# A hybrid decoder layer: where two of the five sums of output-weight quarters are made, and the ticks that space the others

## The chip, the cores and the metric

The program runs on one core of one Trainium2 chip. The metric is the device time of one execution in microseconds, taken as the median of several runs. All data is float32; every large product is made of three TensorE matmuls, because each operand is split into a high part (rounded to float32r) and a low part (the rest).

## What is computed

One decoder layer on 1024 positions of width 2048, cut to the parts that matter here:

```python
xn = rms_norm(x, norm_w)
proj = xn @ w_in                      # 2048 x 7184, cut into head groups A and B
o_a = group_a(proj)                   # gated delta rule, 8 heads of 128
o_b = u_b * chunked_causal_sgu(layer_norm(v_b), w_s, b_s) * silu(z_b)   # 8 groups of 128
mix = concatenate([o_a, o_b]) @ w_out # 2048 x 2048
out = rms_norm(x + mix, final_norm_w)
```

## The kernel before

**Stages.** The 1024 positions are worked in two halves of 512. For each half comes group A (projections, convolution, and the recurrence in pairs of heads) and then group B: three blocks of the v projection (`vb`), and then sixteen projections of 128 columns, u and z in turn. A projection is four loads of `w_in` (tile `wr`, 256 KB each), each split by ScalarE (`wh`, line 135) and VectorE (`wl`, line 136), and 48 matmuls into `acc` (lines 237, 238 and 240). After both halves comes the output phase.

**The output phase** makes the last product with seven block products in place of eight (Strassen's scheme): the table `PRODUCTS` gives for each of the seven the quarters of the mixed activations that are added, the quarters of `w_out` that are added, and the blocks of the result that it goes into. Each product has two column halves (`cb`) of eight steps `k`; a step has one weight tile `wro` of 256 KB (split into `who`, `wlo`) and twelve matmuls into `oa` (lines 970 to 972). With `cb` 0 a step also loads and splits the activations (`ar` or `as`, then `a`). At the end of each column half, VectorE adds four accumulators into one or two result blocks each (line 908, `c`); the first time that a block is written it adds the residual `xres`, which is loaded into the tile tag `z` (two buffers).

**The sums.** Five of the seven products (0, 2, 3, 4 and 6) need a sum or a difference of two quarters of `w_out`. `w_sums` (line 828 on) makes them during group B, 80 units of 128 by 512, 40 in each half. A unit loads two tiles (`wsa`, `wsb`, lines 834 and 835; tags `cv` with three buffers and `bv` with two), adds them on VectorE (line 842) and stores the sum in DRAM through POOL's queue (`wc_d`, line 843). The output phase later loads `wro` from `wc_d`, for products 1 and 5 from `w_out` itself.

**What sets the order.** A list of tasks (Python generators) is stepped by `tick()`, two ticks per load of `w_in`; each `yield n` waits n ticks. `run` holds four weight tiles prepared ahead. The framework then lays out each engine's instructions when the program is built: a row can stand before others that were written earlier. Loads and most stores are issued by SP in that fixed order, and an issue whose buffer isn't free holds all behind it. `swap` for the output of a head (`nc.gpsimd`) goes through POOL's queue: four stores (`swapo`, line 429), then one load back (`ut`, line 432), on which VectorE waits in line 671 (`o`).

Constants that the change touches: `W_SWO` (ticks between the swap of a pair's output and line 671), `W_SUM0` (ticks before the first unit), and the number in `w_sums`' `yield 3`.

Of the kernel before, what the change touches and what calls it, by code (L numbers as in the profile page):

```python
# [8 lines left out]
F32 = mybir.dt.float32  # L9
# [8 lines left out]
P = 128  # L18
DM = 2048
SEQ = 1024  # L20
T = 512
NHALF = SEQ // T
KT = DM // P
# [8 lines left out]
def kernel(ctx, tc, x_tok, x_t, w_in, w_v0, w_vb, w_out, conv_w, norm_w, a_log, dt_bias,  # L32
                       hn_w, sgu_w, sgu_b, wsp_t, b_sp, fn_w, out):
    nc = tc.nc
# [5 lines left out]
    wk = pool("wk", bufs=2)  # L40
    sm = pool("sm", bufs=2)
    dr = pool("dr", bufs=2, space=DRAM)
# [72 lines left out]
    tt = cst.tile([P, 2 * NT, P], F32, name="tt")  # L115
    nc.gpsimd.memset(tt, 0.0)

    wc_d = dr.tile([5, 2, KT // 2, P, T], F32, name="wc_d", bufs=1)
    mix_d = [dr.tile([2 * H, P, T], F32, name=f"mix_d{i}", bufs=1) for i in range(NHALF)]


# [11 lines left out]
    def split(hi, lo, src):  # L133

        nc.scalar.copy(hi, src)  # L135
        nc.vector.tensor_tensor(lo, src, hi.bitcast(F32), op=ALU.subtract)  # L136
# [43 lines left out]
        nc.scalar.copy(rb, rp)  # L180
        return rb

    def w_chunk(src, shape, name, keep=None, raw=None):
        if raw is None:
            raw = wp.tile(shape, F32, tag="wr", bufs=3, name=f"wr{name}")
        nc.sync.dma_start(raw, src)
        hi, lo = keep or (wp.tile(shape, F32R, tag="wh", name=f"wh{name}"), wp.tile(shape, F32R, tag="wl", name=f"wl{name}"))
        split(hi, lo, raw)
        return hi, lo
# [7 lines left out]
    def spawn(gen):  # L197
        n = next(gen, None)
        if n is not None:
            tasks.append([n, gen])  # L200
# [29 lines left out]
    def w_tile(hf, ct, q):  # L230
        return w_chunk(w_in[ct, :, q * KH:(q + 1) * KH, :], [P, KH, P], f"{hf}_{ct}_{q}")
# [29 lines left out]
    def first_tiles(hf, xs, env, done):  # L261
# [3 lines left out]
        for q in range(KT // 2):  # L265
            def prep(q=q):
                ks = slice(2 * q, 2 * q + 2)
                raw = wp.tile([P, 2, 2, P], F32, tag="wr", bufs=3, name=f"wrf{hf}_{q}")
                hi = wp.tile([P, 2, 2, P], F32R, tag="wh", name=f"whf{hf}_{q}")
                lo = wp.tile([P, 2, 2, P], F32R, tag="wl", name=f"wlf{hf}_{q}")  # L270
                sqs_, sqs[:] = list(sqs), []
                for i in range(2):
                    x, sq = x_load(hf, 2 * q + i)
                    xs.append(x)
                    sqs.append(sq)
                    nc.sync.dma_start(raw[:, i], w_in[(H, 0)[i], :, ks, :])
                    split(hi[:, i], lo[:, i], raw[:, i])
                if q % 3 == 0:
                    vraw.append(big.tile([P, 3, 2, 288], F32, tag="b8", name=f"v0r{hf}_{q}"))
                v2 = big.tile([P, 2, 2, 288], F32R, tag="b8", name=f"v0{hf}_{q}")[:, :, :, 0:V0]  # L280
                vb = w_chunk(w_v0[q], None, None, (v2[:, 0], v2[:, 1]), vraw[-1][:, q % 3, :, 0:V0])
                for sq in sqs_ + (sqs if q == KT // 2 - 1 else []):
                    sq()
                if hf == 0 and q == 5:
                    conv_constants()
                return hi, lo, vb
# [154 lines left out]
        return s4  # L441


    W_SWO = 20
    W_SO0 = 4
    W_CONV = 7
    W_SWAP = 7
# [6 lines left out]
    W_GATES = 12  # L454
    W_LN = 12
    W_EM = 5
    W_SUM0 = 30

    def task_k(hf, h, st, pr, acc):
        gt, hh = st["gt"], h % 2  # L460
# [87 lines left out]
    def task_pair(hf, p, st, pr):  # L548
# [95 lines left out]
        for h2, hd in enumerate(heads):  # L644
# [19 lines left out]
            yield 1  # L664
        yield W_SWO
        while not all("z" in hd for hd in heads):
# [100 lines left out]
    def group_b(hf, xs, st):  # L767

        env, sb = {}, {}
        units = [(n, cb, k) for n in SUMS for cb in range(2) for k in range(HK)]  # L770
        spawn(w_sums(units[hf * len(units) // 2:(hf + 1) * len(units) // 2]))
        for blk in range(1, 4):
            for k2 in range(KT // 2):
# [34 lines left out]
    PRODUCTS = (  # L808
# [7 lines left out]
    )  # L816
    SUMS = [n for n, pr in enumerate(PRODUCTS) if len(pr[1]) > 1]
    KEPT = ((0, 0), (1, 1))
    ASLOTS = [tb for tag, bufs in (("kd", 3), ("gae", 3), ("wq", 2), ("bv", 2), ("o", 2), ("ut", 2), ("kc", 2))
              for tb in [(tag, bufs)] * bufs]  # L820
    op = {1: ALU.add, -1: ALU.subtract}

    def w_quarter(b, cb, k):

        return w_out[b[1] * 2 + cb, b[0] * HK + k]

    def w_sums(units):

        def load(u):
            n, cb, k = u  # L830
            a, b, _ = PRODUCTS[n][1]
            ta = wk.tile([P, 1, T], F32, tag="cv", bufs=3, name=f"wsa{n}_{cb}_{k}")
            tb = wk.tile([P, 1, T], F32, tag="bv", bufs=2, name=f"wsb{n}_{cb}_{k}")
            nc.sync.dma_start(ta, w_quarter(a, cb, k))
            nc.sync.dma_start(tb, w_quarter(b, cb, k))
            return ta, tb
        yield W_SUM0
        nxt = load(units[0])
        for i, (n, cb, k) in enumerate(units):
            (ta, tb), nxt = nxt, (load(units[i + 1]) if i + 1 < len(units) else None)  # L840
            yield 3
            nc.vector.tensor_tensor(ta, ta, tb, op=op[PRODUCTS[n][1][2]])  # L842
            nc.gpsimd.dma_start(wc_d[SUMS.index(n), cb, k], ta.rearrange("p o c -> p (o c)"))

    def out_phase():
# [29 lines left out]
        def a_prep(n, k):  # L875
            spec = PRODUCTS[n][0]
            src = a_raw(n, spec[0], k)
            if len(spec) > 1:
                dst = src if spec[0] not in KEPT else wk.tile([P, T], F32, tag="cv", bufs=3, name=f"as{n}_{k}")
                nc.vector.tensor_tensor(dst, src, a_raw(n, spec[1], k), op=op[spec[2]])  # L880
                src = dst
            hi, lo = (wk.tile([P, T], F32R, tag=tag, bufs=bufs, name=f"a{i}{n}_{k}")
                      for i, (tag, bufs) in enumerate(ASLOTS[2 * k:2 * k + 2]))
            split(hi, lo, src)
            return hi, lo

        def prep(n, cb, k):
            src = w_quarter(PRODUCTS[n][1][0], cb, k) if n not in SUMS else \
                wc_d[SUMS.index(n), cb, k].rearrange("p (o c) -> p o c", o=1)
            keep = None  # L890
            if n == LAST and cb == 1 and k < HK - 4:
                keep = [act.tile([P, 1, T], F32R, tag="ah", name=f"wk{i}_{k}") for i in range(2)]
            w = w_chunk(src, [P, 1, T], f"o{n}_{cb}_{k}", keep)
            if cb == 0:
                return w, a_prep(n, k)
            return w, None
# [153 lines left out]
```

## Time and profile before

| | |
|---|---|
| median of 3 runs | 1821.09 us (1820.3 to 1825.88) |
| the profiled execution | 1825.52 us, its span 1823.4 us |
| mean granted TensorE clock | 0.989 |
| PE busy | 1739.9 us, 95% |
| VectorE (DVE) busy | 1267.0 us, 69% |
| ScalarE (ACT) busy | 733.3 us, 40% |
| group B, sixteen projections | 536.3 to 754 us, and 1287.1 to 1504.4 us |
| output phase | 1504.4 to 1823.4 us |

The profile is one execution. Busy time of PE counts a matmul at whatever clock it ran, so a stretch can be fully busy and still be slow; the granted clock stands beside it in the views by stretch. The difference of 2.1 us between the execution's time and its span lies outside the program's instructions.

### The profile page before, as it was taken

Reading aid. Unit: us, or ns where it says so; the run is one execution under the profiler, and the core shown is the slowest. Engines: PE = TensorE matmul, PEld = TensorE weight load, DVE = VectorE, ACT = ScalarE, POOL = GpSimd, SP = SyncE. Lnnn points to the kernel's source line nnn. Section 1 sums busy time; section 2 is a strip of 40 time slices with the busy share of each in tenths; the row PEclk is TensorE's granted clock in tenths of the full one; section 3 lists DMA queues with packets and bytes.
Section 4 is the critical chain, followed back from the end, with each engine's and each line's share of the span. In section 5 each row is a group of like instructions: output and inputs, shape, how many; then the busy total and the mean of one; then the engine's idle time right before and its main releaser. Section 6 shows DMA issues by size and latency. Waiting matters only on the chain. (4 is left out here: it accounts for less than half of the span.)

```text
span 1823.4 us, 27717 instructions
## 1 busy us (share of the span) xinstructions
PE 1739.9 (95%) x9334; PEld 1460.5 (80%) x9334; DVE 1267.0 (69%) x2985; ACT 733.3 (40%) x1670; POOL 307.0 (17%) x394
## 2 busy tenths in 40 slices
PE   9999999999987989999999999999888999999997
PEld 8778788887986768887888878799766788778886
DVE  7797797978556643757979888684664445675785
ACT  6544435444232222637344454432421233333453
POOL 4210121311212310203012012120141000110121
PEclk9999999999999999999999999999999999999999
DMA  7455454454568884426443635444888557643564
GB/s 241 117 137 141 105 146 123 107 159 120 141 208 300 285 254 125 127 65 172 127 131 96 171 93 153 125 126 116 280 291 271 170 165 239 204 138 100 172 220 144
DMA packets 197599, 301.07 MB, mean 165 GB/s; under 512 B 39472, under 2 KB 72272, under 8 KB 197200
## 3 DMA queue, kind: packets, MB, share of 16 engines
q1 hardware_dynamic: 186368, 265.69, 50.3%
q0 software_dynamic: 10944, 33.60, 5.7%
q8 instruction: 73, 1.20, 0.3%
q14 instruction: 70, 0.57, 0.1%
q10 hardware_dynamic: 144, 0.01, 0.0%
HBM read 241.51 MB, written 57.70 MB: 164 GB/s over the span
## 5 line engine op out<-in xcount | busy, mean ns | idle before, releaser
L240 PE MATMUL acc<-xh,wl 128*128 128x512 f32 x1472 | 582.0, 395 | 27.4 <-DVE wl L136 27.4
L237 PE MATMUL acc<-xh,wh 128*128 128x512 f32 x1472 | 594.2, 404 | 0.9 <-ACT wh L135 0.9
L238 PE MATMUL acc<-xl,wh 128*128 128x512 f32 x1472 | 578.6, 393 | 0.0
L135 ACT CAST wh<-wr 128x512 fp32r<-128x512 f32 x368 | 225.8, 617 | 460.4 <-PE acc L238 212.3
L240 PEld LDWEIGHTS acc<-xh,wl 128*128 128x128 f32 x1472 | 278.8, 189 | 93.4 <-DVE wl L136 34.8
L136 DVE TENSOR_TENSOR wl<-wr,wh 128x512 fp32r<-128x512 f32 x368 | 255.1, 696 | 109.1 <-ACT wh L135 105.9
L237 PEld LDWEIGHTS acc<-xh,wh 128*128 128x128 f32 x1472 | 279.2, 190 | 58.2 <-issue 3.2
L238 PEld LDWEIGHTS acc<-xl,wh 128*128 128x128 f32 x1472 | 279.2, 190 | 52.4 <-issue 0.2
L971 PE MATMUL oa<-wlo,a 128*128 128x512 f32 x432 | 168.6, 390 | 3.3 <-DVE wlo L136 3.3
L972 PE MATMUL oa<-who,a 128*128 128x512 f32 x432 | 168.2, 389 | 0.0
L970 PE MATMUL oa<-who,a 128*128 128x512 f32 x432 | 168.2, 389 | 0.0
L842 DVE TENSOR_TENSOR wsa<-wsa,wsb 128x512 f32<-128x512 f32 x80 | 58.2, 728 | 97.9 <-DMA wsb<-w_out 53.8
L412 DVE SCALAR_TENSOR_TENSOR cv<-pc,cw,cv 128x511 f32<-128x511 f32 (+1 forms) x144 | 108.6, 754 | 8.4 <-ACT cv L409 6.8
L788 PE MATMUL vb<-whvb,xh 128*128 128x256 f32 x384 | 111.2, 290 | 0.0
L136 DVE TENSOR_TENSOR wlo<-wro,who 128x512 fp32r<-128x512 f32 x108 | 80.6, 750 | 43.8 <-ACT who L135 43.7
L788 PE MATMUL vb<-wlvb,xh 128*128 128x256 f32 x384 | 109.2, 284 | 0.0
L788 PE MATMUL vb<-whvb,xl 128*128 128x256 f32 x384 | 109.2, 284 | 0.0
L135 ACT CAST who<-wro 128x512 fp32r<-128x512 f32 x108 | 66.5, 617 | 82.0 <-PE oa L972 44.1
L971 PEld LDWEIGHTS oa<-wlo,a 128*128 128x128 f32 x432 | 81.1, 188 | 21.9 <-DVE wlo L136 5.0
L972 PEld LDWEIGHTS oa<-who,a 128*128 128x128 f32 x432 | 81.1, 188 | 16.7
L970 PEld LDWEIGHTS oa<-who,a 128*128 128x128 f32 x432 | 81.1, 188 | 16.7
L565 DVE TENSOR_TENSOR fst<-fs 32x31 f32<-32x31 f32 (+15 forms) x248 | 90.1, 363 | 4.2
(246 smaller groups left out, 2564.6 us busy)
## 6 DMA issues: line engine op xcount, KB each, us to landing
wr<-w_in SPq DMA_DIRECT2D x368, 256.0 KB, 3.5
wsa<-w_out SPq DMA_DIRECT2D x80, 256.0 KB, 4.2
wsb<-w_out SPq DMA_DIRECT2D x80, 256.0 KB, 4.2
wc_d<-wsa POOLq DMA_DIRECT2D x80, 256.0 KB, 4.6
wro<-wc_d SPq DMA_DIRECT2D x80, 256.0 KB, 2.7
wrvb<-w_vb SPq DMA_DIRECT2D x48, 256.0 KB, 2.7
ar<-mix_d SPq DMA_DIRECT2D x48, 256.0 KB, 3.7
xr<-x_t SPq DMA_DIRECT2D x32, 256.0 KB, 3.8
```

The lines of the kernel that those rows point to most:

```text
L135: nc.scalar.copy(hi, src)
L136: nc.vector.tensor_tensor(lo, src, hi.bitcast(F32), op=ALU.subtract)
L237: nc.tensor.matmul(acc, hi[:, kk, :], xh, start=(k == 0), stop=False)
L238: nc.tensor.matmul(acc, hi[:, kk, :], xl, start=False, stop=(last and lo is None))
L240: nc.tensor.matmul(acc, lo[:, kk, :], xh, start=False, stop=last)
L412: nc.vector.scalar_tensor_tensor(cv[:, s:], acc[:, :T - s], w, cv[:, s:], op0=ALU.mult, op1=ALU.add)
L565: nc.vector.tensor_tensor(tv, bc(lu[:, k, k + 1:].unsqueeze(2), [32, n, m]), bc(xu[:, k:k + 1, 0:m], [32, n, m]), op=ALU.mult)
L788: nc.tensor.matmul(a, l[:, tsl], r[:, k % 2, :], start=fl, stop=sp_, skip_group_check=True)
L842: nc.vector.tensor_tensor(ta, ta, tb, op=op[PRODUCTS[n][1][2]])
L970: nc.tensor.matmul(acc[t], ah[:, tsl], hi[:, 0, :], start=(k == 0), stop=False)
L971: nc.tensor.matmul(acc[t], ah[:, tsl], lo[:, 0, :], start=False, stop=False)
L972: nc.tensor.matmul(acc[t], al[:, tsl], hi[:, 0, :], start=False, stop=(k == HK - 1))
```

## The change

Products 3 and 4 no longer have their sums made in group B. `SUMS` is now (0, 2, 6): 48 units, 24 in each half, and `wc_d` has three sums in place of five. In the output phase, for the 32 weight tiles of products 3 and 4, `prep` loads both quarters from `w_out` (`wro` and a new tile `wb`, which has the tag `z` for product 3 and `cv` for product 4), and VectorE adds the second to the first just ahead of the split. The task of the sums waits 18 ticks in place of 30 at its start, and 6 in place of 3 between units; `W_SWO` is 26 in place of 20.

```diff
-    wc_d = dr.tile([5, 2, KT // 2, P, T], F32, name="wc_d", bufs=1)
+    wc_d = dr.tile([3, 2, KT // 2, P, T], F32, name="wc_d", bufs=1)
...
-    def w_chunk(src, shape, name, keep=None, raw=None):
+    def w_chunk(src, shape, name, keep=None, raw=None, add=None):
...
         nc.sync.dma_start(raw, src)
+        if add:
+            nc.vector.tensor_tensor(raw, raw, add[0], op=add[1])
         hi, lo = keep or (wp.tile(shape, F32R, tag="wh", name=f"wh{name}"), wp.tile(shape, F32R, tag="wl", name=f"wl{name}"))
         split(hi, lo, raw)
...
-    W_SWO = 20
+    W_SWO = 26
...
-    W_SUM0 = 30
+    W_SUM0 = 18
...
-    SUMS = [n for n, pr in enumerate(PRODUCTS) if len(pr[1]) > 1]
+    SUMS = (0, 2, 6)
+    SUMB = {3: ("z", 2), 4: ("cv", 3)}
...
-            yield 3
+            yield 6
...
-            w = w_chunk(src, [P, 1, T], f"o{n}_{cb}_{k}", keep)
+            add = None
+            if n in SUMB:
+                tag, bufs = SUMB[n]
+                add = wk.tile([P, 1, T], F32, tag=tag, bufs=bufs, name=f"wb{n}_{cb}_{k}")
+                nc.sync.dma_start(add, w_quarter(PRODUCTS[n][1][1], cb, k))
+                add = add, op[PRODUCTS[n][1][2]]
+            w = w_chunk(src, [P, 1, T], f"o{n}_{cb}_{k}", keep, add=add)
```

The rows below show the built order. In a name such as `wsa2_1_0` stand the product, the column half and the step; in `wr0_42_1` the half of the positions, the column tile of `w_in` and the quarter of its load. The last number is the framework's own.

SP's queue in group B of the first half, at the loads for column tile 40, before:

```order
L186 DMA wr0_40_0_6029<-w_in 128x512
L835 DMA wsb0_0_6_5720<-w_out 128x512
L834 DMA wsa0_0_6_5719<-w_out 128x512
L835 DMA wsb0_0_7_5801<-w_out 128x512
L186 DMA wr0_40_1_6069<-w_in 128x512
L834 DMA wsa0_0_7_5800<-w_out 128x512
L835 DMA wsb0_1_0_5879<-w_out 128x512
L834 DMA wsa0_1_0_5878<-w_out 128x512
L834 DMA wsa0_1_1_5990<-w_out 128x512
L835 DMA wsb0_1_1_5991<-w_out 128x512
L186 DMA wr0_40_2_6109<-w_in 128x512
L186 DMA wr0_40_3_6143<-w_in 128x512
```

The same place with the change:

```order
L186 DMA wr0_40_0_6017<-w_in 128x512
L840 DMA wsb0_0_6_5795<-w_out 128x512
L839 DMA wsa0_0_6_5794<-w_out 128x512
L186 DMA wr0_40_1_6051<-w_in 128x512
L840 DMA wsb0_0_7_5979<-w_out 128x512
L839 DMA wsa0_0_7_5978<-w_out 128x512
L840 DMA wsb0_1_0_6088<-w_out 128x512
L839 DMA wsa0_1_0_6087<-w_out 128x512
L839 DMA wsa0_1_1_6217<-w_out 128x512
L186 DMA wr0_40_2_6091<-w_in 128x512
L840 DMA wsb0_1_1_6218<-w_out 128x512
L186 DMA wr0_40_3_6125<-w_in 128x512
```

The eight loads of sums between the first and the last weight load of this tile are the same eight; two weight loads moved one row forward.

SP's queue some 55 rows on, where the 24th unit of the first half ends, before:

```order
L186 DMA wr0_34_3_6549<-w_in 128x512
L834 DMA wsa2_0_7_6666<-w_out 128x512
L835 DMA wsb2_0_7_6667<-w_out 128x512
L835 DMA wsb2_1_0_6703<-w_out 128x512
L186 DMA wr0_42_0_6574<-w_in 128x512
L834 DMA wsa2_1_0_6702<-w_out 128x512
L834 DMA wsa2_1_1_6739<-w_out 128x512
L835 DMA wsb2_1_1_6740<-w_out 128x512
L186 DMA wr0_42_1_6598<-w_in 128x512
L834 DMA wsa2_1_2_6784<-w_out 128x512
L186 DMA wr0_42_2_6616<-w_in 128x512
```

The same place with the change:

```order
L186 DMA wr0_34_3_6507<-w_in 128x512
L839 DMA wsa2_0_7_7213<-w_out 128x512
L840 DMA wsb2_0_7_7214<-w_out 128x512
L186 DMA wr0_42_0_6526<-w_in 128x512
L145 DMA xr1_0_7479<-x_t 128x512
L145 DMA xr1_5_7567<-x_t 128x512
L186 DMA wr0_42_1_6550<-w_in 128x512
L145 DMA xr1_10_7743<-x_t 128x512
L186 DMA wr0_42_2_6568<-w_in 128x512
```

After the 24th unit the queue holds no more loads of sums in this half; three loads of the next half's input (`xr`) moved up. In the second half the same place holds loads of `ar`.

VectorE's queue in the output phase, at the change from product 3 to product 4, before:

```order
L136 TENSOR_TENSOR wlo4_0_3_16716<-wro4_0_3_16713,who4_0_3_16715 128x512
L908 TENSOR_TENSOR c00_1_15764<-c00_1_15764,oa3_1_2_16553 128x512
L908 TENSOR_TENSOR c11_5_15363<-c11_5_15363,oa3_1_2_16553 128x512
L908 TENSOR_TENSOR c00_1_15764<-c00_1_15764,oa3_1_3_16554 128x512
L908 TENSOR_TENSOR c11_7_15365<-c11_7_15365,oa3_1_3_16554 128x512
L136 TENSOR_TENSOR wlo4_0_4_16746<-wro4_0_4_16743,who4_0_4_16745 128x512
L136 TENSOR_TENSOR a14_7_16816<-ar11_7_16116,a04_7_16815 128x512
L136 TENSOR_TENSOR wlo4_0_5_16768<-wro4_0_5_16765,who4_0_5_16767 128x512
L136 TENSOR_TENSOR wlo4_0_6_16790<-wro4_0_6_16787,who4_0_6_16789 128x512
```

The same place with the change, from the last of those accumulators on:

```order
L919 TENSOR_TENSOR c11_7_15173<-c11_7_15173,oa3_1_3_16398 128x512
L188 TENSOR_TENSOR wro4_0_4_16613<-wro4_0_4_16613,wb4_0_4_16611 128x512
L188 TENSOR_TENSOR wro4_0_5_16638<-wro4_0_5_16638,wb4_0_5_16636 128x512
L188 TENSOR_TENSOR wro4_0_6_16663<-wro4_0_6_16663,wb4_0_6_16661 128x512
L136 TENSOR_TENSOR wlo4_0_4_16617<-wro4_0_4_16613,who4_0_4_16616 128x512
L136 TENSOR_TENSOR wlo4_0_5_16642<-wro4_0_5_16638,who4_0_5_16641 128x512
L136 TENSOR_TENSOR a14_7_16696<-ar11_7_15924,a04_7_16695 128x512
L136 TENSOR_TENSOR wlo4_0_6_16667<-wro4_0_6_16663,who4_0_6_16666 128x512
L188 TENSOR_TENSOR wro4_0_7_16688<-wro4_0_7_16688,wb4_0_7_16686 128x512
L188 TENSOR_TENSOR wro4_1_0_16713<-wro4_1_0_16713,wb4_1_0_16711 128x512
L136 TENSOR_TENSOR wlo4_0_7_16692<-wro4_0_7_16688,who4_0_7_16691 128x512
L188 TENSOR_TENSOR wro4_1_1_16734<-wro4_1_1_16734,wb4_1_1_16732 128x512
```

Three additions now stand between the accumulators and the next split, and from there on an addition for a tile two steps ahead follows each split.

## Rows read from the trace of the kernel before

**Rows 1.** The page's first line.

```profile
span 1823.4 us, 27717 instructions
```

**Rows 2.** Stretches (start:end, length): busy PE, PEld, DVE, ACT, POOL (records); clock, DMA, GB/s.

```profile
536.30:615.30 79.00, 67.65 (x330) 55.68 (x329) 53.59 (x133) 24.43 (x62) 23.62 (x33) 0.96 0.88 291
615.30:676.50 61.20, 50.47 (x209) 39.52 (x208) 26.11 (x41) 10.77 (x18) 13.07 (x20) 0.94 0.87 276
676.50:721.80 45.30, 45.30 (x209) 37.82 (x208) 18.57 (x27) 12.37 (x20) 2.58 (x2) 1.00 0.48 136
...
1366.00:1426.50 60.50, 49.57 (x210) 38.41 (x209) 25.51 (x39) 10.19 (x17) 12.24 (x17) 0.97 0.80 263
1426.50:1471.80 45.30, 45.30 (x210) 37.80 (x209) 17.64 (x26) 11.87 (x20) 3.65 (x4) 1.00 0.51 146
```

**Rows 3.** PE's waits in 615.3:676.5 (first row) and in 453:615.3: total, times, longest.

```profile
PE acc L240 <- DVE wl L136: 10.7, 5, 3.5
...
PE at L648 <- DVE s L745: 8.7, 1, 8.7
PE ds L631 <- DVE vz L623: 3.3, 2, 2.5
PE p L620 <- DVE va L724: 2.2, 1, 2.2
```

**Rows 4.** Timeline of VectorE, 606 to 636: start, duration, idle before and what ended it.

```profile
611.01 0.69 DVE L842 TENSOR_TENSOR wsa<-wsa,wsb 128x512 f32<-128x512 f32 x1 [1.73 <-DMA wsb<-w_out]
611.62 0.75 DVE L745 SCALAR_TENSOR_TENSOR s<-sp,lnw,brow 128x512 f32<-128x512 f32 x1
...
623.44 0.75 DVE L671 SCALAR_TENSOR_TENSOR o<-ut,hnw,z 128x512 f32<-128x512 f32 x1 [6.90 <-DMA ut<-swapo]
...
635.24 0.69 DVE L842 TENSOR_TENSOR wsa<-wsa,wsb 128x512 f32<-128x512 f32 x1 [5.35 <-DMA wsb<-w_out]
```

**Rows 5.** Timeline of POOL, 612 to 615.

```profile
612.45 1.70 POOL L748 TENSOR_TENSOR s<-s,rb 128x512 f32<-128x512 f32 x1 [5.30 <-DVE s L745]
614.09 0.76 POOL L429 DMA_DIRECT2D swapo<-ut  x1
```

**Rows 6.** DMA issues, median us to landing: 620:676, 675:745, 1640:1725 (two rows).

```profile
wr<-w_in SPq DMA_DIRECT2D x15, 256.0 KB, 4.7
...
wr<-w_in SPq DMA_DIRECT2D x25, 256.0 KB, 3.1
...
wro<-wc_d SPq DMA_DIRECT2D x26, 256.0 KB, 2.6
...
wro<-w_out SPq DMA_DIRECT2D x5, 256.0 KB, 3.5
```

**Rows 7.** Stretches of products 1 to 5 of the output phase, columns as in group 2.

```profile
1547.90:1593.90 46.00, 44.40 (x193) 35.83 (x193) 32.78 (x49) 16.31 (x32) 5.76 (x4) 1.00 0.68 208
1593.90:1639.50 45.60, 43.86 (x193) 35.98 (x193) 34.07 (x50) 17.26 (x33) 5.94 (x4) 1.00 0.46 133
1639.50:1683.10 43.60, 43.60 (x194) 36.10 (x193) 24.68 (x40) 14.20 (x25) 0.00 (x0) 1.00 0.38 108
1683.10:1726.60 43.50, 43.50 (x194) 36.03 (x193) 29.87 (x53) 16.63 (x32) 5.90 (x4) 1.00 0.51 157
1726.60:1770.10 43.50, 43.50 (x194) 36.03 (x193) 36.59 (x86) 26.33 (x52) 5.39 (x4) 1.00 0.75 243
```

**Rows 8.** Timeline of VectorE in product 3, 1656 to 1663.

```profile
1656.70 0.69 DVE L136 TENSOR_TENSOR wlo<-wro,who 128x512 fp32r<-128x512 f32 x1 [2.03 <-ACT who L135]
...
1660.03 2.48 DVE L908 TENSOR_TENSOR c<-c,oa 128x512 f32<-128x512 f32 x4
```

**Rows 9.** Shorter stretches around column tiles 34 and 42 of half 1, 42 and 35 of half 2.

```profile
604.30:615.30 11.00, 11.00 (x52) 9.12 (x51) 7.68 (x12) 3.04 (x5) 5.66 (x7) 1.00 0.84 267
615.30:632.30 17.00, 13.50 (x56) 10.87 (x55) 7.69 (x12) 2.48 (x4) 4.68 (x8) 0.90 0.87 276
...
1366.00:1393.90 27.90, 23.67 (x106) 18.73 (x105) 12.38 (x18) 4.70 (x8) 5.39 (x8) 1.00 0.83 272
```

## The prediction

> **What bounds the kernel now.** I read the table of stretches first, cut where a projection begins, because the page's 95% busy PE is a mean over stages and counts a matmul at half clock as busy. The span is 1823.4 us [rows 1]. The table has two kinds of stretch for the same work. Four projections with nothing beside them (676.5 to 721.8, and 1426.5 to 1471.8) take 45.3 us at a granted clock of 1.00, with PE busy for all of it [rows 2]. The four projections just ahead of them, with the same count of matmul records (209 and 210), take 61.2 and 60.5 us [rows 2]. So the kernel is bound by PE nearly everywhere, except in group B while the sums are made: there the reader is to see that PE, VectorE and ScalarE are all idle for part of the time while the DMA engines show 0.80 to 0.88. The list of PE's waits says what it waits for: the low half of a split weight, 10.7 us in five waits [rows 3]. The other part of the 15.9 us lost is clock: the mean grant there is 0.94 [rows 2], which is time at the 1.2 GHz level behind such waits.
>
> The timeline of VectorE names the cause. Its queue is in order, a sum stands in it ahead of a split, and the sum waits for its loads: 5.35 us at 635 [rows 4]. The weight loads themselves land in 4.7 us there and in 3.1 us once the sums are over [rows 6].
>
> **The change part by part.** *Removed from group B: 32 units, 16 in each half.* A unit is two loads, an addition and a store. The diff says that the rest is spaced at six ticks. The built order says otherwise: between the weight loads of column tile 40 there are the same eight loads of sums as before, since the framework brings them forward as far as buffers allow, and the 24th unit stands at the same place. What changes is what comes behind it: in the first half no load of a sum from the first load for tile 42 on, where before there were 16 units more, down to tile 36. These four projections (42, 35, 43, 36) are exactly the stretch of 61.2 us, and of 60.5 us in the second half [rows 2]. I take it that they will run as the four behind them do now, with the same splits, evacuations and weight loads and no sums: 61.2 - 45.3 = 15.9 us and 60.5 - 45.3 = 15.2 us, **31.1 us** in all. The clock is in these numbers, since both rows are times.
>
> *Left in group B: 24 units in each half.* The stretch ahead (536.3 to 615.3) takes 79.0 us, with PE busy 67.65 [rows 2]. Its longest wait is 8.7 us, PE behind VectorE, which waits in line 671 for a swap [rows 3]; the rows of VectorE and POOL around that place keep their order, so I leave it at its price. `W_SWO` is written six ticks later, but line 671 keeps its place in VectorE's queue: nothing. The smaller reordering (weight loads and splits one row ahead of a sum) touches the waits of 3.3 and 2.2 us of the recurrence [rows 3]. They could go or double: 0, between 6 us less and 6 us more in each half; I count half of that to each side for both together, 6 us.
>
> *Moved by the freed queue.* Loads of the next stage (`xr`, `ar`) are issued earlier. They wait for nothing in that stretch and fill buffers that the sums held: nothing. The 32 stores leave POOL's queue, where the swaps stand behind them; that can only help, and is part of the 15.9 and 15.2 us.
>
> *Added to the output phase: 32 additions and 32 more loads.* The loads of `wro` were 32 from `wc_d` and are now 64 from `w_out`. An addition of this size steps at 0.60 us where VectorE is not held up: four evacuations take 2.48 us, the last of them some 0.68 [rows 8]. Twelve of product 3's additions and four of product 4's fall in product 3's stretch: 24.68 + 16 x 0.60 = 34.3 us busy of 43.6, 79%. In product 4's stretch it is 29.87 + 12 x 0.60 = 37.1 of 43.5, 85%. Product 5 has 36.59 of 43.5 now, 84%, and PE is never idle in it [rows 7]. So VectorE has the room; the idle time that hides the additions is its wait of 2.03 us for ScalarE ahead of each split [rows 8]. Room is not all: products 1 and 2 lose 1.6 and 1.7 us to late splits at 71% and 75%, where evacuations and additions bunch [rows 7]. The change bunches likewise (three additions behind eight evacuations at product 4's start). By count, a split there comes 4 x 0.60 + 3 x 0.60 + 0.60 = 4.8 us behind the one before it, against 43.5 / 16 = 2.72 us for a step of PE, and four tiles are held ahead. I take one such stall, **+1.7 us**, with 0 as the lower end.
>
> *The pairing of loads* bounds it from above. `wr` has three buffers: the load of tile k+3 can start once the split of tile k is done, then it lands, is added and is split as soon as its turn comes, so two tiles take at least one landing and two steps of VectorE (0.69 us each, by the split's row [rows 8]). The landing is 3.5 us for the few loads of `w_out` in the stretch of products 3 and 4, where DMA is 0.38 to 0.51 [rows 6, 7]: (3.5 + 1.4) / 2 = 2.45 us per tile, under PE's 2.72. At the 4.7 us of the crowded stretch [rows 6] it is 3.05, or 0.33 x 32 = **10.6 us** more. I take the row of 3.5, which is nearest in place and load; the 10.6 us go into the range.
>
> The Trainium skill (DMA: Bandwidth & Descriptors, "Anatomy of one DMA") gives a fixed cost near 2.0 us and bytes over 436 GB/s; for 256 KB that is an estimate of 2.6 us, and by it the pair costs (2.6 + 1.4) / 2 = 2.0 us per tile, nothing. The trace agrees for loads of `wc_d` in the quiet stretch (2.6 us), and not for the crowded one (4.7 us).
>
> **The sum.** -31.1 + 1.7 = -29.4 us against the profiled execution's 1825.52, so 1796.1 for a run like that one. It lies 4.4 us above the median of the runs, 1821.09; against the median the forecast is **1791.7 us**. If those 4.4 us lay in the stretch that goes, the gain from the median is 25.0 and the time 1796.1.
>
> **The rivals.**
>
> *The swap takes the place of the sums.* In the first half VectorE waits 6.90 us in line 671 at 623 for the second head's swap, just ahead of the split that PE then lacks [rows 4]. That wait stays in the order. If it still holds PE, tile 42 keeps its excess: a projection of its kind is 45.3 / 2 - 11.0 = 11.7 us (a pair less the 11.0 of the other kind), so 17.0 - 11.7 = 5.3 us; in the second half the pair of 27.9 us keeps 27.9 - 22.65 = 5.25 us [rows 9]. The gain is then 10.6 less: 1821.1 - 31.1 + 10.6 + 1.7 = 1802 us. Against it: the swap is late because its fourth store stands on POOL behind line 748, which waits 5.30 us for VectorE's line 745 [rows 5], and that one came at 611.62 behind sums that waited for loads, one of them 1.73 us [rows 4]. Those sums are among the 16 that go.
>
> *The output phase becomes bound by its pairs of loads.* With the mechanism above, 4.7 us gives 1821.1 - 31.1 + 10.6 = 1801 us. It ends slower than before where the 32 tiles lose more than 31.1 us, 0.97 us each, that is at 3.69 us per tile, or a landing of 2 x 3.69 - 1.4 = 6.0 us. At 6.5 us it is 3.95 per tile, 39.4 us more: 1829 us. For it: twice the loads on one in-order queue, each behind its own buffer, with residual loads and the outputs on the same queue. Against it: DMA shows 0.38 and 0.51 there, and 4.2 MB more in each product's 43.5 us are 96 GB/s on 108 and 157 [rows 7], still no more than the 276 GB/s at which 4.7 us was seen.
>
> *The spacing works as it is written.* If the sums that stay are in truth spread over twice the time, the stretch of 79.0 us is relieved as well. PE is idle there for 11.35 us in the first half [rows 2], and I take the same for the second: 1791.7 - 22.7 = 1769 us. The rows of SP's order speak against it.
>
> **How the numbers follow.** The forecast 0.70; the swap 0.14; the pairs of loads 0.10, of which 0.05 slower than before; the spacing 0.06. The range starts 10 us under the forecast (6 us for the reordered waits, and part of the last rival) and ends where the swap's case and the forecast with crowded loads lie, with the 4.4 us of the profiled run: 1782 to 1806. About 0.3% is what a measurement here can tell from no change, 5.5 us. Faster by more than that: 0.93; within: 0.02; slower: 0.05.
>
> **What would show it.** The four projections from tile 42 on last 45 to 47 us in both halves at clock 1.00, with no wait of PE on a split; the stretch ahead stays near 79 us with its 8.7 us wait; products 3 and 4 last 43.5 us each, up to 2 more, with VectorE near 80 and 85%. The forecast is wrong if line 671 still holds the split of tile 42, if the splits of products 3 and 4 wait for landings, or if the stretch of the 24 units that stay has grown.

## The result

The changed kernel takes **1802.26 us** in the median of 4 runs (1797.79 to 1808.93), beside 1823.49 us for the kernel before (1820.3 to 1827.67): ratio 0.9885, 95% interval 0.9846 to 0.9925. Measured once more it was 1801.08 us (5 runs) beside 1823.66, ratio 0.9874 (0.9852 to 0.9897). So it is faster by 21 to 23 us where 29.4 were forecast, and the time lies 10.6 us above the forecast of 1791.7 and inside its range. Of the 10.6 us, 2.4 are the reference, whose median was 1823.49 in this comparison and 1821.09 in the one that the prediction started from; 8.2 us are gain that did not come.

The profiled execution of the changed kernel took 1797.79 us, the shortest of its runs; its span is 1796.1 us.

The table of stretches, cut where a projection begins. Columns: start:end, length; busy PE, PEld, DVE, ACT, POOL with records; granted clock, DMA share, GB/s. The first two rows and the last two are the places of [rows 2], half 1 and half 2.

```profile
537.10:621.10 84.00, 70.05 (x329) 57.24 (x328) 53.11 (x131) 25.48 (x65) 23.01 (x32) 0.92 0.85 274
621.10:666.50 45.40, 45.40 (x210) 37.86 (x210) 19.04 (x26) 11.27 (x19) 4.43 (x4) 1.00 0.42 117
...
1273.60:1351.80 78.20, 68.06 (x329) 55.99 (x328) 52.39 (x130) 23.76 (x62) 23.18 (x32) 0.96 0.82 273
1351.80:1397.10 45.30, 45.30 (x209) 37.82 (x208) 19.38 (x26) 11.10 (x18) 4.81 (x4) 1.00 0.42 118
```

The four projections from tile 42 on went from 61.2 and 60.5 us to 45.4 and 45.3, with PE busy for all of it at a clock of 1.00 and the DMA share halved. The five ahead of them (tiles 32, 40, 33, 41 and 34), which keep their 24 units, went from 79.0 to 84.0 us in half 1; PE's busy time there rose from 67.65 to 70.05 us for the same matmuls because more of them ran at the lower clock level (0.92 in place of 0.96). In half 2 they take 78.2 us. PE's waits between 453 and 621 us, to be held against [rows 3]:

```profile
PE at L650 <- DVE s L747: 10.2, 1, 10.2
PE ds L633 <- DVE vz L625: 3.2, 4, 1.6
PE p L622 <- DVE va L726: 2.8, 1, 2.8
```

The 10.7 us behind `wl` are gone, and the list for 621 to 711 us is empty. The long wait at the swap is 10.2 us where it was 8.7 (lines have moved by two: 650 is 648 before).

The stretches of products 0 to 6 of the output phase; the middle five answer to [rows 7]:

```profile
1475.10:1518.70 43.60, 43.60 (x194) 36.10 (x193) 24.21 (x39) 14.83 (x26) 0.54 (x1) 1.00 0.76 239
1518.70:1564.30 45.60, 44.13 (x194) 35.97 (x193) 31.61 (x48) 15.75 (x32) 5.72 (x4) 1.00 0.71 204
1564.30:1610.20 45.90, 43.86 (x194) 35.99 (x193) 37.74 (x55) 17.86 (x35) 5.95 (x4) 1.00 0.53 159
1610.20:1653.80 43.60, 43.60 (x194) 36.08 (x194) 33.12 (x53) 14.23 (x25) 0.00 (x0) 1.00 0.67 200
1653.80:1697.40 43.60, 43.60 (x194) 36.12 (x193) 34.99 (x61) 15.76 (x30) 5.99 (x4) 1.00 0.68 213
1697.40:1743.10 45.70, 44.12 (x194) 35.93 (x193) 39.51 (x92) 27.68 (x54) 5.63 (x4) 1.00 0.76 249
1743.10:1786.70 43.60, 43.30 (x192) 35.52 (x190) 29.91 (x74) 19.75 (x42) 11.21 (x8) 1.00 0.39 125
```

Products 3 and 4, which now make their sums beside their splits, take 43.6 us each as before, with VectorE at 33.12 and 34.99 us of it. Product 5, which has no sum of its own, takes 45.7 where it took 43.5.

### The profile page after: what moved, and what is told of

The parts are those of the page before. It is cut to its first block, busy times and chain, and to the rows that moved or that the text cites. A ratio compares the mean times of both kernels' runs of the same rounds, so it can differ in the third digit from the quotient of the medians.

```text
span 1796.1 us, 27540 instructions
## 1 busy us (share of the span) xinstructions
PE 1731.5 (96%) x9334; PEld 1458.4 (81%) x9334; DVE 1271.1 (71%) x2985; ACT 734.2 (41%) x1670; POOL 290.2 (16%) x362
## 4 chain that ended last, share of the span: by engine, by line
PE 66%; DVE 14%; DMA 11%; issue 4%; ACT 3%; POOL 1%; SPq 1%; DVEq 0%; ACTq 0%; POOLq 0%
PE acc L239 13%; PE acc L242 12%; PE acc L240 12%; PE vb L790 7%; PE oa L983 4%; PE oa L982 4%; PE oa L981 4%; DVE wl L136 2%; DMA wsb<-w_out 2%; DVE cv L414 2%; DMA xres<-x_tok 2%; DMA wc_d<-wsa 2%; DMA ar<-mix_d 1%; DMA pc<-swapk 1%; DVE fs L569 1%
## 5 line engine op out<-in xcount | busy, mean ns | idle before, releaser
L136 DVE TENSOR_TENSOR wl<-wr,wh 128x512 fp32r<-128x512 f32 x368 | 260.9, 712 | 139.1 <-ACT wh L135 137.6
L569 DVE TENSOR_TENSOR fs<-fs,fst 32x31 f32<-32x31 f32 (+15 forms) x248 | 89.6, 361 | 4.1
```

The costliest lines, as they stand in the source:

```text
L569: nc.vector.tensor_tensor(xu[:, k + 1:, 0:m], xu[:, k + 1:, 0:m], tv, op=ALU.subtract)
```

## The experiments

**The tick numbers put back: is the missing gain theirs?** The move without the new spacing:

```diff
-    W_SWO = 26
+    W_SWO = 20
-    W_SUM0 = 18
+    W_SUM0 = 30
-            yield 6
+            yield 3
```

> The changed kernel with the three tick numbers set back (18 to 30, 6 to 3, 26 to 20), so that only the move of products 3 and 4 is left. Theory 1 (the sums stand as early as buffers allow, whatever the ticks say): as the changed kernel, 1802 us within 6; the four projections from tile 42 on again 45.3 us in both halves, the stretch ahead again 78 to 84 us. Theory 2 (the spacing does a part of it): over 1810 us, since the 24 units of a half would again bunch at the old rate and the stretch of 79 us would grow.

1790.87 us (1789.1 to 1799.2), ratio 0.9837 (0.9804 to 0.987) against 1823.15: 32.3 us under the kernel before, and below what either theory had. That is 11 us better than the changed kernel, but not measured beside it. So both were run again side by side:

> The changed kernel itself, beside the next run on the same chip. Theory T (the changed tick numbers cost time: a few splits, weight loads and matmuls of tiles 32, 40, 33 and 41 stand in another order): about 1800 us, with the stretch from tile 32 to tile 42 at 80 to 84 us in the first half. Theory N (the 11 us between the changed kernel and the one with the old ticks are scatter from run to run): the two come out within 4 us of each other.

> The changed kernel with the tick numbers of before (W_SUM0 30, yield 3, W_SWO 20), beside the run above. Theory T: 1789 to 1793 us, 7 to 13 us under the changed kernel on this chip, stretch from tile 32 to tile 42 at 78 to 80 us in both halves. Theory N: within 4 us of the changed kernel.

The changed kernel 1801.08 us (1796.51 to 1803.41, 5 runs), the old ticks 1796.27 (1795.02 to 1800.64, 4 runs); ratios 0.9874 (0.9852 to 0.9897) and 0.9858 (0.9834 to 0.9881). 4.8 us, between the two theories, with runs that overlap. The stretch from tile 32 to tile 42, half 1 and half 2, of the first run with old ticks, of its repetition, and of the changed kernel's repetition:

```profile
534.60:613.20 78.60, 67.50 (x330) 55.58 (x329) 53.07 (x131) 24.70 (x63) 23.14 (x32) 0.96 0.87 283
1267.60:1343.80 76.20, 67.57 (x329) 55.54 (x329) 52.11 (x130) 23.69 (x61) 23.17 (x32) 0.96 0.85 277
```

```profile
540.30:616.80 76.50, 67.43 (x328) 55.82 (x328) 51.83 (x128) 24.25 (x62) 22.66 (x32) 0.95 0.85 284
1274.30:1356.40 82.10, 70.34 (x330) 58.06 (x329) 51.63 (x130) 23.91 (x62) 23.74 (x33) 0.90 0.82 263
```

```profile
533.00:617.20 84.20, 68.93 (x329) 56.73 (x329) 53.13 (x131) 25.54 (x66) 23.09 (x33) 0.92 0.84 272
1272.90:1355.60 82.70, 69.60 (x330) 57.00 (x329) 52.42 (x130) 23.89 (x61) 23.16 (x32) 0.94 0.83 262
```

With the old numbers the stretch takes 79.0 us in [rows 2] and 78.9 us in half 2 of the kernel before (1287.1 to 1366.0), then 78.6, 76.2, 76.5 and 82.1: a mean of 78.6. With the new ones 84.0, 78.2, 84.2 and 82.7: a mean of 82.3. The difference is 3.7 us a half, 7.5 in both. It stands in half 1, where every profile with the new numbers is longer than every one with the old (84.0 and 84.2 against 79.0, 78.6 and 76.5 us); in half 2 the two kinds overlap. Two runs further down, with the new numbers and 32 units a half, agree: 82.8 and 84.9 us in half 1, 83.3 and 81.8 in half 2.

But the stretch is not all that the numbers touch. The first sums are made during the projections of v ahead of it, and there the new numbers are the faster ones. The changed kernel's repetition, then the old ticks beside it:

```profile
451.40:533.00 81.60, 78.75 (x702) 77.81 (x700) 44.48 (x114) 25.36 (x58) 12.85 (x18) 1.00 0.54 160
1192.00:1272.90 80.90, 78.72 (x700) 77.76 (x700) 44.03 (x109) 25.30 (x59) 12.46 (x18) 1.00 0.52 149
```

```profile
455.50:540.30 84.80, 80.16 (x700) 79.01 (x700) 45.96 (x118) 26.74 (x62) 13.32 (x19) 0.98 0.55 166
1191.70:1274.30 82.60, 80.04 (x700) 79.22 (x700) 44.18 (x109) 25.52 (x59) 12.45 (x18) 0.98 0.50 148
```

Over two profiles of each kind the mean is 81.6 against 83.6 us, so some 4 us of the 7.5 come back and about 4 of loss are left. By whole runs the loss is 4.8 us side by side and 11 not side by side. All 9 runs of the changed kernel together average 1801.3 us, all 8 with the old numbers 1794.8: 6.5 us, with an interval of roughly 2 to 11. That the numbers cost time is shown; the size is known no closer than that.

**The additions on GpSimd, in the kernel before: is it VectorE's work or the loads?**

```diff
-            nc.vector.tensor_tensor(ta, ta, tb, op=op[PRODUCTS[n][1][2]])
+            nc.gpsimd.tensor_tensor(ta, ta, tb, op=op[PRODUCTS[n][1][2]])
```

> The kernel before, its 80 additions on POOL in place of VectorE (line 842 alone); loads and stores as before. Theory A (PE lacks splits because a sum that waits for its loads stands ahead of the split in VectorE's in-order queue): most of the 31 us that the two stretches of 61 us lose comes back, so 1795 us or less, and VectorE's waits on loads of w_out vanish with PE's waits on line 136. Theory B (the loads themselves crowd the DMA engines and SP's queue, so that weight loads land late whoever adds): 1823 us within 8, weight loads still land in 4.5 us or more, PE still waits some 10 us in each of these stretches.

1846.01 us (1842.44 to 1848.85), ratio 1.013 (1.0099 to 1.016), slower than either theory had it. PE's longest waits over the span:

```profile
PE at L648 <- DVE s L745: 16.9, 2, 8.8
PE acc L240 <- DVE wl L136: 16.8, 5, 6.5
PE acc L237 <- ACT wh L135: 16.3, 10, 6.2
```

VectorE is rid of the additions, and PE's waits on its half of a split only fall from 27.4 us over the span to 16.8; waits of 16.3 us on ScalarE's half, which reads the loaded tile and stands behind no sum on its own queue, join them. Between 515 and 680 us VectorE waited 48.6 us for loads of sums in the kernel before; here ScalarE waits 71.8 us for weight loads, where it waited 55.6. So the wait that the prediction named can be taken away without the time coming back. An addition takes 1.29 us on GpSimd, where it took 0.69 on VectorE, so it holds its buffers for longer, and VectorE's splits lengthen beside it: 10 of the 37 in this window take more than 0.75 us, 2 of 40 in the kernel before. This run does not separate these from the DMA traffic, and what a sum costs apart from its place in VectorE's queue stays open.

**The loads truly spaced.** In both kernels the loads of a sum are brought forward as far as buffers allow. Here they are tied to the splits: GpSimd writes one column of each buffer from the newest split weight ahead of the load, which then can't start earlier. The changed kernel so, with `W_SUM0` 44 and `yield 5`:

```diff
+        newest[0] = lo
...
+            for t_ in (ta, tb):
+                nc.gpsimd.tensor_copy(t_[:, 0, 0:1], newest[0][:, 0, 0:1].bitcast(F32))
             nc.sync.dma_start(ta, w_quarter(a, cb, k))
```

> The changed kernel with the spacing made real: a one-column copy on POOL from the newest split weight tile into both load tiles holds each unit's loads until that weight has come (five ticks apart, from tick 44). Same sums, same places in the output phase. Theory 1 (what is left in group B is lost to the burst of the 24 units): the stretch from tile 32 to tile 42, 78 to 84 us with the change, falls to 66 to 70 us in both halves, the 10 us wait of PE ahead of line 650 goes, and the time is 1770 to 1785 us. Rival (the wait is the swap's own way through POOL's queue and DRAM, burst or not): the stretch stays at 75 us or more, time 1795 to 1805 us.

1789.0 us (1785.03 to 1792.03), ratio 0.9816 (0.9788 to 0.9845), between the two theories, as the stretch is. The stretch from tile 32 to tile 42 in both halves, and PE's waits in what is left of group B in half 2:

```profile
530.30:602.60 72.30, 67.49 (x330) 55.65 (x329) 45.16 (x119) 24.33 (x63) 20.66 (x36) 0.98 0.60 187
1262.60:1335.00 72.40, 67.92 (x330) 55.45 (x329) 44.82 (x120) 23.79 (x62) 20.92 (x36) 0.98 0.56 179
```

```profile
PE acc L241 <- DVE wl L136: 8.0, 6, 2.5
```

The stretch gains 10 us a half against the changed kernel, with a DMA share of 0.60 and 0.56 where it had 0.85 and 0.82; most of it comes back as small waits on splits later on. Group B as a whole, the projections of v included, takes 284.9 and 283.5 us here (451.5 to 736.4, and 1184.7 to 1468.2), 289.1 and 284.0 in the changed kernel, and 286.1 and 282.4 with the old ticks alone. In the same comparison the old ticks alone took 1790.87 us, and the intervals overlap. So real spacing gains on the changed kernel, but nothing that these runs can tell from putting the numbers back. The same with all five sums, in the kernel before (`yield 4`):

> The kernel before with all five sums in group B, nothing moved to the output phase, but each unit's loads held in the same way, four ticks apart from tick 30: 40 units spread over the 176 ticks. Theory 1 (it is the burst that costs, not the count): some 40 to 50 us less than the kernel before, 1773 to 1785 us, DMA near 0.65 to 0.75 all through group B. Rival (each unit costs its 1 us of PE wherever it stands): 1815 us or more, with the loss spread over all sixteen projections.

1848.96 us (1845.34 to 1851.61), ratio 1.014 (1.0108 to 1.0172). PE's first waits:

```profile
PE acc L239 <- DVE wl L136: 39.5, 28, 4.5
```

Forty spaced units a half do not fit into group B: their last additions stand at 763.5 and 1532.9 us, behind its ends at 753.5 and 1516.4. The rival is right about the time, but the loss is not spread over all sixteen projections as it had it: 31.8 of the 39.5 us lie in the last eight.

**No sums in group B: what are the 48 units that stay worth?**

```diff
-        spawn(w_sums(units[hf * len(units) // 2:(hf + 1) * len(units) // 2]))
...
+            src = w_quarter(PRODUCTS[n][1][0], cb, k)
```

> Part of the computation is left out: products 0, 2 and 6 read the first quarter alone, so group B has no sums, and the output phase is that of the changed kernel. The price of the 24 units left in each half: if they cost what the 32 moved ones did (31.1 us for 32, so 0.97 us each), 48 units give 47 us and the time 1755 us. If most of the stretch of 79 us is the recurrence's own work, its 8.7 us wait for a swap stays: 68 to 72 us each, and 1768 to 1780 us in all.

1761.91 us (1759.97 to 1762.77), 39.2 us under the changed kernel on the same chip: 0.82 us a unit, where the 32 that the change moved took 0.97. The row of the stretch in half 1:

```profile
530.10:597.60 67.50, 65.67 (x329) 54.27 (x328) 42.02 (x115) 24.95 (x63) 13.86 (x16) 1.00 0.41 119
```

The time lies between the two theories. Without the sums the stretch takes 67.5 us at the full clock, 16.7 less than in the changed kernel on the same chip, so that much of it belonged to the sums and not to the recurrence.

**All five sums in the output phase.**

```diff
-    SUMS = (0, 2, 6)
-    SUMB = {3: ("z", 2), 4: ("cv", 3)}
+    SUMS = ()
+    SUMB = {0: ("cv", 3), 2: ("z", 2), 3: ("z", 2), 4: ("cv", 3), 6: ("z", 2)}
```

> All five sums in the output phase, none in group B. If every unit in group B costs what the 32 moved ones cost, the stretch from tile 32 to tile 42 falls from 78 to 84 us to 65 to 70 us in both halves: 22 to 28 us less. In the output phase product 2 would be busy on VectorE for 34.1 + 16 x 0.60 = 43.7 us of 43.6, and products 1 and 2 lost 1.6 us already at 71 and 75%. Theory F (room by the sum of busy time decides): products 0 and 6 lose up to 2 us each, product 2 up to 4: 1772 to 1782 us. Rival B (bunching decides well under 100%): products 0, 2 and 6 lose 5 us or more each, and the time stays at 1790 us or above.

1781.21 us (1779.91 to 1783.53), ratio 0.9768 (0.9744 to 0.9793): 19.9 us under the changed kernel on the same chip, and the best but for a tie below. PE's longest wait between 500 and 720 us, and the stretches of products 0, 1, 2 and 6:

```profile
PE at L650 <- DVE s L747: 0.6, 1, 0.6
```

```profile
1439.20:1485.60 46.40, 44.42 (x194) 35.81 (x192) 28.61 (x46) 12.51 (x22) 0.54 (x1) 1.00 0.85 277
1485.60:1535.40 49.80, 45.74 (x194) 35.45 (x193) 37.79 (x57) 18.57 (x36) 5.99 (x4) 1.00 0.73 226
1535.40:1586.80 51.40, 47.05 (x194) 37.53 (x193) 42.87 (x65) 18.78 (x35) 5.51 (x4) 0.93 0.67 204
...
1719.70:1772.40 52.70, 47.41 (x192) 37.55 (x190) 42.11 (x88) 21.59 (x44) 12.31 (x8) 0.94 0.51 163
```

Even the wait of 10.2 us behind the swap is 0.6 without sums beside it. The output phase gives 21.6 us back: the four stretches are 2.8, 4.2, 5.5 and 9.1 us longer than in the changed kernel, whose products 0, 1, 2 and 6 took 43.6, 45.6, 45.9 and 43.6. The time is that of theory F, at its upper end, but the losses are not where it put them: product 6 was to lose 2 us at most and lost 9.1, product 1 has no sum and lost 4.2. And products 3 and 4 carry the same 16 additions each for nothing, so the count of additions does not decide. Nor does the time that VectorE waits for the load of an addition (line 188). In product 0, which lost 2.8 us, and in product 3, which lost nothing, it is:

```profile
DVE wro L188 <- DMA wro<-w_out: 9.6, 4, 3.1
```

```profile
DVE wro L188 <- DMA wro<-w_out: 8.5, 7, 2.3
```

In products 2 and 6 it is under 1 us. What stands ahead of PE's longest wait in product 6, on VectorE and on GpSimd, is this:

```profile
1746.13 2.48 DVE L918 TENSOR_TENSOR c<-c,oa 128x512 f32<-128x512 f32 x4
1748.53 2.71 DVE L188 TENSOR_TENSOR wro<-wro,wb 128x512 f32<-128x512 f32 x2
...
1751.53 3.07 DVE L136 TENSOR_TENSOR wlo<-wro,who 128x512 fp32r<-128x512 f32 x2
```

```profile
1747.71 6.34 POOL L932 TENSOR_TENSOR c<-c,fw 128x512 f32<-128x512 f32 x4 [16.40 <-ACT sqh L930]
```

```profile
1752.97 0.80 PE L981 MATMUL oa<-wlo,a 128*128 128x512 f32 x1 [2.00 <-DVE wlo L136]
```

VectorE has no idle time here: four evacuations, two additions, and the split that PE lacks behind them. That is bunching, as rival B has it. It is made worse by GpSimd, which scales finished blocks at the time (line 932): the two additions and the two splits take 2.71 and 3.07 us, where two in a row take 1.29 elsewhere. In this output phase, VectorE's instructions that read two tiles of 128x512 take 0.69 us at most when no such GpSimd instruction runs beside them (264 of them); of 21 that run beside one, 18 take longer, up to 1.78 us. Those that read an accumulator do not lengthen (28 beside one, 0.69 at most). In product 2 there is bunching too: VectorE works without a pause from 1538.6 us to the addition at 1546.53, and PE waits 4.0 us for the cast behind it. Product 1, which has no sum, waits for loads instead: VectorE 4.8 us for residuals (`xres`) and 2.3 for activations (`ar`), ScalarE 10.1 for `wro`. That these are the whole loss of each product was not tried. For the landing of the loads, the issues in products 3 and 4 of the changed kernel (median us to landing):

```profile
wro<-w_out SPq DMA_DIRECT2D x31, 256.0 KB, 3.1
wb<-w_out SPq DMA_DIRECT2D x24, 256.0 KB, 3.1
```

**One of the two sums alone.** Product 3's alone moved, then product 4's alone:

```diff
-    SUMS = (0, 2, 6)
-    SUMB = {3: ("z", 2), 4: ("cv", 3)}
+    SUMS = (0, 2, 4, 6)
+    SUMB = {3: ("z", 2)}
```

```diff
-    SUMS = (0, 2, 6)
-    SUMB = {3: ("z", 2), 4: ("cv", 3)}
+    SUMS = (0, 2, 3, 6)
+    SUMB = {4: ("cv", 3)}
```

> The change with product 3's sum alone moved; product 4's stays in group B. 16 units fewer there, 8 in each half. If every unit costs the same, as 31.1 us for 32 says, the gain is half: 15.6 us, with the changed tick numbers' own price of some 6 us 1808 to 1814 us. If the last units cost nothing until the queue is full, the gain is either all (1800 us) or nothing. Product 5's first half of columns: if its stall of 1 to 2 us comes from product 4's additions, which fall just ahead of it, it takes 21.8 us here.

> The change with product 4's sum alone moved; product 3's stays in group B. Time as for the run above, 1808 to 1814 us, by the count of units. Product 5's first half of columns: 23 to 24 us if product 4's additions delay the splits there, 21.8 us if product 3's do or both are needed.

1812.41 us (1809.81 to 1817.67) and 1812.82 us (1808.6 to 1819.96), beside 1819.62: ratios 0.9963 (0.9945 to 0.9981) and 0.9966 (0.9947 to 0.9985). Both times were forecast, and for product 3 alone the profile shows another way to it. The four projections from tile 42 on, in both halves:

```profile
618.00:668.40 50.40, 46.00 (x210) 37.70 (x209) 21.73 (x32) 11.53 (x20) 6.98 (x8) 1.00 0.62 198
1358.60:1405.00 46.40, 45.75 (x210) 37.85 (x209) 20.67 (x29) 11.31 (x19) 6.06 (x7) 1.00 0.59 188
```

Half of the units gives 24.9 of the 31.1 us there (61.2 - 50.4 and 60.5 - 46.4), far from half. But at six ticks the 32 units that stay no longer fit ahead of the output phase. Three sums of the second half stand on VectorE (line 847) among its work, and the activations behind them come late for PE:

```profile
1524.80 1.35 DVE L847 TENSOR_TENSOR wsa<-wsa,wsb 128x512 f32<-128x512 f32 x2 [5.08 <-DMA wsb<-w_out]
...
1528.49 0.69 DVE L847 TENSOR_TENSOR wsa<-wsa,wsb 128x512 f32<-128x512 f32 x1 [1.74 <-DMA wsb<-w_out]
```

```profile
PE oa L981 <- ACT a L135: 7.9, 1, 7.9
```

That takes back 8 us; that the late sums are its cause is read from the order of the rows, and a run with the old numbers was not made. The stretch ahead takes 82.8 and 83.3 us, 8.2 more than before in both halves: -24.9 + 8 + 8.2 makes -8.7, and -7.2 was measured. Product 4 alone shows the same wait (8.0 us). As to product 5: its first half of columns takes 21.8 us with product 3 alone moved and 24.6 with product 4 alone, so product 4's sum is what delays it. All runs bear this out: the nine profiles in which product 4's sum is moved have 22.6 to 24.6 us there, the four others 21.8. Whether it is the additions is not shown: the second tiles (`wb`) of product 4 share their three buffers (tag `cv`) with product 5's activations, which those of product 3 (tag `z`) do not, and no run changes the tag. In the changed kernel PE's two waits there, and ScalarE's cast that they hang on, are these (the load that the cast waits for stands behind eight stores of outputs on SP's queue, issued from 1705.6 to 1710.8 us):

```profile
1717.10 0.50 PE L981 MATMUL oa<-who,a 128*128 128x512 f32 x1 [0.84 <-ACT a L135]
1718.57 0.50 PE L983 MATMUL oa<-who,a 128*128 128x512 f32 x1 [0.74 <-DVE a L136]
```

```profile
1715.90 0.62 ACT L135 CAST who<-wro 128x512 fp32r<-128x512 f32 x1 [1.99 <-DMA wro<-w_out]
```

**Product 6's sum alone left in group B, truly spaced** (`SUMS = (6,)`, the gate from above, `W_SUM0` 44, `yield 14`):

> Sums 0, 2, 3 and 4 in the output phase; product 6's alone stays in group B, its 8 units in each half spaced by a true gate (their loads wait for the newest split weight) at 14 ticks from tick 44. Against the run with all five in the output phase (1781 us): product 6 loses its 9 us there (24.5 and 28.2 us become 21.8 and 21.9), and the 16 units cost 0.56 us each in group B by the gated run with 48 units (27 us over the run with none): 9.0 us. Theory C (cost by count): no change, 1779 to 1783 us. Theory S (a load now and then into a queue that is not full costs nothing): 1772 to 1775 us.

1780.73 us (1777.81 to 1782.1) beside 1819.62, ratio 0.9791 (0.9771 to 0.981). That ties with all five moved, as theory C has it, though the two were not measured side by side. The rows say less than the tie. Product 6 gives its nine us back (it takes 43.7 us again), and the stretch from tile 32 to tile 42 takes only 1.2 and 2.5 of them:

```profile
532.30:600.50 68.20, 65.68 (x329) 54.20 (x328) 44.54 (x118) 24.39 (x62) 16.14 (x25) 1.00 0.51 152
1253.80:1323.10 69.30, 65.74 (x329) 54.31 (x328) 42.94 (x117) 23.89 (x61) 15.79 (x24) 1.00 0.44 131
```

Group B as a whole takes 540.6 us where it took 536.7 with all five moved, so 16 spaced units cost 3.9 us and not the 9.0 of theory C. Another 3.3 us of the tie stand in group A, ahead of 454.4 us (452.0 there) and between the halves (451.6 against 450.7), where the edit changes nothing. Single executions scatter by that much, so between the two theories this run does not decide.

## Why the prediction came out as it did

**The 31.1 us of the moved units: right, to the tenth.** The stretches fell by 15.8 and 15.2 us, to the 45.3 us of an undisturbed row. With the old tick numbers, which is this step and the stall alone, the whole kernel is 32.3 and 27.4 us faster in two comparisons, about 29.4. That the sums' stretch goes is shown; which part of a sum held the splits is not, since the run with the additions on GpSimd lost time too.

**The swap takes the place of the sums: no.** VectorE still waits 4.60 us for the second head's swap at 624 us (6.90 in [rows 4]), and PE has no wait there: the splits ahead of it are early enough.

**The pairs of loads: no, neither with two sums nor with five.** `wro` and `wb` from `w_out` land in 3.1 us in products 3 and 4 (the rows of loads above), under the 3.5 that was chosen, and PE waits for none of them. By the Trainium skill's formula (DMA: Bandwidth & Descriptors, "Anatomy of one DMA"), which the section gives for DMAs issued through GpSimd while these are issued by SP, the estimate was 2.6 us; these rows do not agree, with 0.5 us more at a DMA share of 0.67. With five sums moved the output phase does lose 21.6 us, but the tiles land hardly later in products 1 and 2 (`wro` 3.2 us, `wb` 2.9), and product 3 waits 8.5 us for `wro` and loses nothing. This rival and the one before had forecast 1801 and 1802 us, which is what was measured; as neither mechanism is in the trace, that is chance.

**The stall of 1.7 us: wrong in place, and right in size by luck.** It was put at the start of product 4 by a count of bunched VectorE instructions, and product 4 has none. Product 5 lost 2.2 us (0.9 in the repetition), behind a weight load; product 4's sum is needed for it. The bunching itself is real, but it costs PE where more sums are moved, in product 6 of the run with all five, and there GpSimd's instructions have a part in it.

**The step that failed: the reordering left in the stretch of 24 units, priced at 0.** The prediction saw that the new ticks move weight loads and splits a row past a sum, named the waits that they touch (line 620 and line 631, now 622 and 633), and took zero with 6 us to either side. The stretch grew, which the prediction had named as a sign of being wrong: by 7.5 us in both halves, of which some 4 come back in the projections of v ahead of it. Whole runs put the price of the new numbers at 4.8 us side by side and at 6.5 (roughly 2 to 11) over all runs. With the 2.4 us of the reference and 0.5 of the stall that makes 1791.7 + 2.4 + 0.5 + 4 to 6.5 = 1799 to 1801, where 1802.3 and 1801.1 were measured; the rest is within the scatter of the runs.

Which of the moved rows costs is open. Of the two waits that were named, the 3.3 us at line 631 lie ahead of 536.3 us, so outside the stretch before the change. In half 1, where the growth is, profiles with the new numbers show 10.2 us behind the swap at line 650 (8.4 to 8.8 with the old, 8.7 before), 2.8 at line 622 (0 to 2.2) and 0.5 to 1.8 at line 633 (0 to 0.2). That makes some 4 us of waiting; the other 2 of the 6 us in half 1 are matmuls at a lower granted clock, 0.92 in place of 0.95 and 0.96.

**"The spacing does nothing" was half right.** For 24 units the framework hoists the loads, and the sums end at the same place. For 32 units in each half the last ones are late by the ticks, and land in the output phase. And enforced spacing, with 24 units a half, takes 10 us off the stretch but leaves the whole kernel where the old numbers put it (1789.0 and 1790.87 us, in one comparison).

## What to carry to other kernels

When a stretch with background work stands beside the same stretch without it, the difference of the two rows is the price of that work, clock included, and it held here to the tenth of a microsecond. It is the price of all of it at once: half of the units gone gave 24.9 of the 31.1 us. A number that reorders rows by one place in a stretch that is already starved is not free, even where no single wait seems to depend on it: run the move with and without it, and look at the neighbouring stretches too, where a part of the loss may come back. A delay written in scheduling steps does not space anything by itself when the builder brings loads forward. A load tied to data is spaced, but judge the spacing by the whole stage and not by the stretch that it relieves.

## What was not expected of the hardware

A sum's two loads and its addition cost nothing in products 3 and 4, where the DMA share is 0.67 and 0.68, and 2.2 us for all 32 in product 5 behind them; with its store a unit costs 0.82 us in group B, at a share of 0.82 to 0.85. The share alone does not tell the two apart: with all five sums moved, product 2 lost 5.5 us at 0.67 and product 6 lost 9.1 at 0.51. The recurrence's long wait behind its swap, 8.7 us before, is 0.6 us with no sums beside it: it was part of the price of the sums, though its row names only the swap. And VectorE's instructions on two tiles slowed beside GpSimd's, from 0.69 us to as much as 1.78, while those that read an accumulator did not.
